# Seven norms of a transformer layer: column sums of width one, or wide sums with a tile of ones

## The chip, the cores and the metric

The kernel runs on one core of a Trainium2 chip. The metric is device time in microseconds. The kernel before takes 1665.77 us, the median of three runs (1663.8, 1665.77 and 1667.88). One further execution was recorded by the profiler: it took 1668.83 us, of which 1665.7 us are the span that the trace covers.

Matrix products run on PE, weights are loaded into it by PEld, elementwise work with two tensors runs on DVE, activations and copies on ACT, a little elementwise work on POOL, and most transfers are issued by SP. Each engine works through its own list of instructions in order; an instruction that waits holds up all that stand behind it on that engine.

## The reference

One encoder layer is applied to two requests with the same weights: a prompt of 512 tokens and a sample of 1024 tokens, both of width 1024, all in fp32. What matters here:

```python
def _rmsnorm(x, g):
    y = x * rsqrt(mean(x * x, axis=-1) + 1e-6) * g

h = _rmsnorm(x, g_pre_mix) * (1 + scale_a) + shift_a
q, k, v, u = split(h @ w_in)
mix = concat(attention(q, k, v), pool(u)) @ w_out
x = x + gate_a * _rmsnorm(mix, g_post_mix)          # the mixer norm
h = _rmsnorm(x, g_pre_mlp) * (1 + scale_m) + shift_m # the norm ahead of feed-forward
x = x + gate_m * _rmsnorm(relu(h @ w_ff1) ** 2 @ w_ff2, g_post_mlp)  # the norm after feed-forward
```

The mean of each norm goes over the 1024 channels of one token.

## The kernel before

Activations are held transposed: a tile has 128 channels on its partitions and 512 tokens along the free dimension, so one half of a request (`c` is 0 for the prompt, 1 for the sample; `hf` is the half, and only the sample has two) is eight such tiles. Since channels lie on partitions, the sum of squares of a token runs across partitions, and PE forms it.

The squares of eight tiles are either added up on DVE first (into `ss`, with the eighth square kept apart as `sq`, so two tiles reach PE), or, in the second norm of the prompt's mixer, handed to PE one by one (eight tiles, there named `x`).

A norm then goes like this. `square_sums` (L195) takes each of the four 128-token slices of a tile as the stationary operand and multiplies it by one column of the tile of ones, so that four matmuls of width one put 512 sums into a 128x4 tile `nv_m`, tokens on partitions. `rsqrt_small` (L163) makes the inverse root of these 128x4 numbers with two activations (`rs_u`, L170 and L171) and four small DVE operations (L172 to L175). `norm_sums` (L177) brings the result back across partitions: four matmuls of 128x128 against the identity write it into `nv_r`, a 128x512 tile in PSUM in which every partition holds the same row (L186), and ACT copies it into SBUF as `nv_R` (L191). With `keep` the copy is left out and the users read PSUM. DVE multiplies the activations by that tile.

The program passes through these stages:

- To about 280 us: the prompt's input projection with its own first norm, the sample's first norms and input projection, the prompt's attention in between.
- From about 290 to 860 us the sample's attention runs in the background. In front of it are the prompt's output projection, the prompt's two mixer norms (`out_post(0, 0)`, 342 to 391 us), and the prompt's feed-forward.
- At 904 us the norm after the prompt's feed-forward (`finish` with `c` 0). The sample's output projection for both halves follows to about 1004 us; `out_post(1, 0)` with its two norms lies inside (953 and 979 us).
- From about 1000 us the sample's first feed-forward product (`ff1_s`), with `out_post(1, 1)` and its two norms (1004 and 1030 us) inside. The second of them is followed by `combine_h`, a long run of elementwise work that makes the operands of a Strassen-like product from both halves.
- To the end: the rest of the feed-forward and the sample's last norms (`finish` with `c` 1), which the change leaves as they are.

A scheduler sets the order in which the instructions of the woven stages stand on each engine. It goes by the order of writing, by priorities and by its own costs. Buffers of a tag are shared in a ring of fixed length: `sq`, `ss` and `nv_R` have two each, the PSUM tile `m` of the norms has one.

Of the kernel before, what the change touches and what calls it, by code (L numbers as in the profile page):

```python
# [7 lines left out]
F32 = mybir.dt.float32  # L8
# [4 lines left out]
AL = mybir.AluOpType  # L13
# [3 lines left out]
KB = 8  # L17
NFB = 32
EPS = 1e-6

V_GPM, V_GQM, V_GPL, V_GQL, V_PS, V_B, V_C = 0, 8, 16, 24, 32, 36, 84
NV = 100
# [24 lines left out]
def hymba_encoder_layer(ctx, tc, xp, xs, ns_, vec, gqk, rope, edge, ident_in, w_ada_c,  # L47
# [129 lines left out]
    def norm_sums(m, keep=False):  # L177

        n = m.shape[1]
        rs = st_p.tile([128, n], F32, tag="nv_rs", name="nv_rs")
        rsqrt_small(rs, m, 1024.0, [128, n], "nv_")
        r = ps_m.tile([128, n * 128], F32, tag="m", name="nv_r")
        for j in range(n):
            nc.tensor.matmul(r[:, j * 128:(j + 1) * 128], lhsT=rs[:, j:j + 1].to_broadcast([128, 128]),  # L186
                             rhs=ident, start=True, stop=True)
        if keep:
            return r
        rt = st_p.tile([128, n * 128], F32, tag="nv_R", name="nv_R")  # L190
        nc.scalar.activation(out=rt, in_=r, func=AF.Copy)  # L191
        return rt

    def square_sums(m, sq, first, last):

        n = m.shape[1]
        for j in range(n):
            nc.tensor.matmul(m[:, j:j + 1], lhsT=sq[:, j * 128:(j + 1) * 128], rhs=ones[:, 0:1],  # L198
                             start=first and j == 0, stop=last and j == n - 1)

    def sums_tile(n=4):
        return ps_m.tile([128, 512], F32, tag="m", name="nv_m")[:, 0:n]

    def norm_vec(sqs, keep=False):

        m = sums_tile(sqs[0].shape[1] // 128)
        for i, sq in enumerate(sqs):
            square_sums(m, sq, i == 0, i == len(sqs) - 1)
        return norm_sums(m, keep)

    def sumsq_add(ss, src, m, eng):

# [546 lines left out]

    def out_post(c, hf):  # L760
        sl = slice(hf * 512, (hf + 1) * 512)
        R = norm_vec(ss_t[c, hf])
        yield
        sqs = []
        if c == 0:
            sums = sums_tile()
        else:
            ss = st_p.tile([128, 512], F32, tag="ss", name="ss2")
        for m in range(KB):
            mx = acc[c, hf][m]  # L770
            xt = land()
            dma(xt, X[c][m, :, sl])
            nc.vector.scalar_tensor_tensor(mx, mx, gg_mix[:, m, c:c + 1], R, op0=AL.mult, op1=AL.mult)
            nc.vector.tensor_tensor(mx, mx, xt, AL.add)
            put(x1_d[c][m, :, sl], mx)
            if c == 0:
                nc.scalar.activation(out=xt, in_=mx, func=AF.Square)
                sqs.append(xt)
                if m > 1:
                    square_sums(sums, sqs[m - 2], m == 2, False)  # L780
            else:
                sq = sumsq_add(ss, mx, m, nc.vector)
            yield
        if c == 0:
            for m in (KB - 2, KB - 1):
                square_sums(sums, sqs[m], False, m == KB - 1)
            R2 = norm_sums(sums)
        else:
            R2 = norm_vec([ss, sq])
        yield  # L790
        if c == 1 and hf == 1:
            yield from combine_h(R2)
            return
        for m, (hh, hl) in enumerate(hi_lo(c, hf)):
            modulate(acc[c, hf][m], R2, a_mlp[:, m, c:c + 1], mod[:, 24 + m, c:c + 1], hh, hl, full=c == 1)
            yield
# [428 lines left out]
    def finish(c, hf, sqs, t0=0, n=512, lands=4):  # L1225
# [8 lines left out]
            dma(xts[m].rearrange("p (m t) -> p m t", m=g), x1_d[c][m:m + g, :, sl].rearrange("m p t -> p m t"))  # L1234
        for m in steps[:lands]:
            load(m)
        R = norm_vec(sqs, True)
        yield
        for m in steps:
            if m not in xts:  # L1240
# [261 lines left out]
```

## Time and profile before

| What | Before |
|---|---|
| median of three runs | 1665.77 us |
| the profiled execution, its own time | 1668.83 us |
| its span in the trace | 1665.7 us |
| PE busy | 1611.2 us, 97% |
| PEld busy | 1299.9 us, 78% |
| DVE busy | 1213.7 us, 73% |
| ACT busy | 854.8 us, 51% |
| mean granted clock of PE | 0.984 |

Busy time is the time in which an engine had an instruction at work. A matmul is recorded with its full length although the next one starts before it ends, so the time that a matmul takes on a busy PE is read from start to start in the timeline, not from its length. A matmul of two fp32 operands is recorded as two instructions, which is why four of them stand as x8. The granted clock is the share of full speed at which PE ran. Waits are put down to the instruction that came last.

### The profile page before, as it was taken

The page shows a single profiled execution, that of the slowest core. Times are in us where ns is not written, and L with a number is a line of the kernel's source. Part 1 is how long each engine was busy: PE and PEld are TensorE (multiplying, and loading weights), DVE is VectorE, ACT ScalarE, POOL GpSimd, SP SyncE. Part 2 cuts the span into 40 slices and gives each one's busy share as a digit, 9 for nine tenths or more (in the row PEclk, how much of TensorE's full clock was granted, in tenths as well). Part 3 has the DMA queues.
Part 4 walks back from the last instruction along what each step waited for, and adds up shares of the span by engine and source line. Part 5 has one row for each costly group of instructions (what it writes and reads, how often), then busy time and mean ns, then how long its engine had stood idle before and what let it go on. Part 6 is the DMA issues. An engine that isn't in the chain of part 4 may idle for free. (4 is left out here: it accounts for less than half of the span.)

```text
span 1665.7 us, 21550 instructions
## 1 busy us (share of the span) xinstructions
PE 1611.2 (97%) x7680; PEld 1299.9 (78%) x7680; DVE 1213.7 (73%) x1938; ACT 854.8 (51%) x1450; POOL 10.4 (1%) x27
## 2 busy tenths in 40 slices
PE   7999998999999999999999999899999999999996
PEld 4467886788888878888888888788888788888886
DVE  7898988568667675655667487878875576878757
ACT  2446664556645545546453475744445564444433
POOL 0000000000000000000000000000000000000002
PEclk8999999989999999999999999999999999999998
DMA  7756776443555553332368537566663745444334
GB/s 294 279 156 186 224 221 183 146 153 123 166 174 180 165 179 102 100 108 89 99 206 245 178 127 246 195 224 226 225 216 121 237 160 186 140 141 152 93 110 152
DMA packets 150618, 287.57 MB, mean 173 GB/s; under 512 B 15152, under 2 KB 56432, under 8 KB 150512
## 3 DMA queue, kind: packets, MB, share of 16 engines
q1 hardware_dynamic: 125824, 258.31, 47.9%
q10 hardware_dynamic: 24688, 27.89, 5.4%
q8 instruction: 60, 0.98, 0.2%
q14 instruction: 46, 0.38, 0.1%
HBM read 223.20 MB, written 61.37 MB: 171 GB/s over the span
## 5 line engine op out<-in xcount | busy, mean ns | idle before, releaser
L140 DVE TENSOR_TENSOR wl<-raw,wh 128x1024 fp32r<-128x1024 f32 (+2 forms) x106 | 121.1, 1142 | 70.4 <-ACT wh L139 69.9
L139 ACT ACTIVATE wh<-raw 128x1024 fp32r<-128x1024 f32 (+2 forms) x106 | 105.4, 995 | 120.4 <-PE mm L160 91.7
L630 ACT ACTIVATE p<-s,amx 128x1024 f32<-128x1024 f32 (+1 forms) x96 | 93.3, 972 | 108.6 <-DVE amx L628 106.7
L657 DVE TENSOR_TENSOR pl<-pT,ph 128x512 fp32r<-128x512 f32 x160 | 108.6, 686 | 54.8 <-ACT ph L656 54.3
L875 PE MATMUL pa<-fo,wh 128*128 128x512 f32 x448 | 140.4, 395 | 2.7 <-ACT x L1012 2.7
L628 DVE TENSOR_REDUCE amx<-s 128x1 f32<-128x1024 f32 (+1 forms) x96 | 100.1, 1042 | 43.5 <-PE s L618 43.1
L656 ACT ACTIVATE ph<-pT 128x512 fp32r<-128x512 f32 x160 | 93.4, 594 | 46.1 <-PE pT L653 36.8
L159 PE MATMUL mm<-hA,wh 128*128 128x512 f32 x256 | 106.7, 417 | 0.0
L159 PE MATMUL mm<-fh,wh 128*128 128x512 f32 x256 | 106.5, 417 | 0.0
L875 PE MATMUL mm<-fo,wh 128*128 128x512 f32 x336 | 104.8, 393 | 0.0
L875 PEld LDWEIGHTS pa<-fo,wh 128*128 128x128 f32 x448 | 84.8, 189 | 21.9 <-ACT x L1012 3.1
L161 PE MATMUL mm<-fh,wl 128*128 128x512 f32 x256 | 101.3, 396 | 0.0
L160 PE MATMUL mm<-fl,wh 128*128 128x512 f32 x256 | 101.0, 394 | 0.0
L160 PE MATMUL mm<-hA,wh 128*128 128x512 f32 x256 | 100.9, 395 | 0.0
L161 PE MATMUL mm<-hA,wl 128*128 128x512 f32 x256 | 100.5, 394 | 0.0
L653 PE MATMUL pT<-ident,p 128*128 128x128 f32 x640 | 96.6, 275 | 1.4 <-DVE pl L657 0.9
L618 PE MATMUL s<-kst,q 128*128 128x512 f32 x320 | 93.9, 406 | 4.0 <-ACT p L630 2.0
L653 PEld LDWEIGHTS pT<-ident,p 128*128 128x128 f32 x640 | 79.3, 142 | 22.6 <-issue 2.4
L875 PE MATMUL pa<-fo,wl 128*128 128x512 f32 x224 | 88.1, 393 | 0.0
L881 ACT ACTIVATE fo<-raw 128x512 fp32r<-128x512 f32 x106 | 66.3, 631 | 38.3 <-DMA raw<-f_d 31.5
L882 DVE TENSOR_TENSOR fo<-raw,fo 128x512 fp32r<-128x512 f32 x106 | 71.2, 689 | 15.8 <-ACT fo L881 15.2
L666 PE MATMUL x<-ph,vst 128*128 128x256 f32 x320 | 81.7, 285 | 0.5 <-ACT ph L656 0.5
(291 smaller groups left out, 3922.5 us busy)
## 6 DMA issues: line engine op xcount, KB each, us to landing
raw<-in_w_ff SPq DMA_DIRECT2D x56, 512.0 KB, 3.8
f_d<-x SPq DMA_DIRECT2D x98, 256.0 KB, 2.8
raw<-f_d SPq DMA_DIRECT2D x98, 256.0 KB, 3.0
raw<-in_w_ada_c SPq DMA_DIRECT2D x40, 512.0 KB, 3.9
g<-in_w_ada_c SPq DMA_DIRECT2D x24, 512.0 KB, 4.3
q<-q_d SPq DMA_DIRECT2D x96, 128.0 KB, 3.6
raw<-in_w_out SPq DMA_DIRECT2D x24, 512.0 KB, 3.8
rawx<-in_w_ff SPq DMA_DIRECT2D x20, 512.0 KB, 4.0
```

Of the source, the lines that this page charges most:

```text
L139: nc.scalar.activation(out=fh, in_=r[:, :n], func=AF.Copy)
L140: nc.vector.tensor_tensor(fl, r[:, :n], fh.bitcast(F32), AL.subtract)
L159: nc.tensor.matmul(ps, lhsT=wh[:, k, :], rhs=ah, start=(i == 0), stop=False)
L160: nc.tensor.matmul(ps, lhsT=wh[:, k, :], rhs=al, start=False, stop=False)
L161: nc.tensor.matmul(ps, lhsT=wl[:, k, :], rhs=ah, start=False, stop=(i == len(ks) - 1))
L618: nc.tensor.matmul(s[:, f * 512:(f + 1) * 512], lhsT=q[:, h, p, :], rhs=kst[c][:, kv, f * 512:(f + 1) * 512].bitcast(F32R), start=(p == 0) ...
L628: nc.vector.tensor_reduce(mx, s[:, :n], AX.X, AL.max, negate=True)
L630: nc.scalar.activation(out=pr, in_=s[:, :n], func=AF.Exp, bias=mx, accum_out=den)
L653: nc.tensor.transpose(t[:, k, :], pr[:, (4 * f + k) * 128:(4 * f + k + 1) * 128], ident)
L656: nc.scalar.activation(out=hi, in_=t, func=AF.Copy)
L657: nc.vector.tensor_tensor(lo, t, hi.bitcast(F32), AL.subtract)
L875: nc.tensor.matmul(ps, lhsT=x[:, k, :], rhs=y, start=start and k == i == 0, stop=k == n - 1 and i == 2, skip_group_check=not start)
```

## The change

Seven norms are formed in another way: both of the prompt's mixer stage (`out_post(0, 0)`), the one after the prompt's feed-forward (`finish` with `c` 0), and the two of each half of the sample (`out_post(1, 0)` and `out_post(1, 1)`). The others keep the old way.

`wide_sums` makes the whole 128x128 tile of ones the stationary operand and streams the tile of squares through PE, 512 columns wide. Each partition of the PSUM tile `nv_w` then holds all 512 sums at once, so nothing has to be brought back across partitions. `wide_norm` makes the inverse root on 128x512 tiles: three activations (Ln, Exp, and an Identity that leaves the mean in SBUF) and three DVE operations, with the same Newton step as before. The result `nv_U` is used where `nv_R` was. These six operations carry a higher priority for the scheduler. The two intermediate tiles come from the ring of `sq`.

```diff
+URGENT = 300
+    def wide_sums(m, sq, first, last):
+        nc.tensor.matmul(m, lhsT=ones, rhs=sq, start=first, stop=last)
+
+    def wide_norm(m):
+        n = m.shape[1]
+        with tc.high_priority(URGENT):
+            u = st_p.tile([128, 512], F32, tag="nv_R", name="nv_U")[:, :n]
+            ms = st_p.tile([128, 512], F32, tag="sq", name="nv_M")[:, :n]
+            t = st_p.tile([128, 512], F32, tag="sq", name="nv_T")[:, :n]
+            nc.scalar.activation(out=u, in_=m, func=AF.Ln, bias=eps_t, scale=1.0 / 1024.0)
+            nc.scalar.activation(out=u, in_=u, func=AF.Exp, scale=-0.5)
+            nc.scalar.activation(out=ms, in_=m, func=AF.Identity, bias=eps_t, scale=1.0 / 1024.0)
+            nc.vector.tensor_tensor(t, u, u, AL.mult)
+            nc.vector.scalar_tensor_tensor(t, t, -0.5, ms, op0=AL.mult, op1=AL.mult)
+            nc.vector.scalar_tensor_tensor(u, t, 1.5, u, op0=AL.add, op1=AL.mult)
+        return u
+
+    def wide_vec(sqs):
+        m = ps_m.tile([128, 512], F32, tag="m", name="nv_w")[:, :sqs[0].shape[1]]
+        for i, sq in enumerate(sqs):
+            wide_sums(m, sq, i == 0, i == len(sqs) - 1)
+        return wide_norm(m)
...
     def out_post(c, hf):
-        R = norm_vec(ss_t[c, hf])
+        R = wide_vec(ss_t[c, hf])
...
-            sums = sums_tile()
+            sums = ps_m.tile([128, 512], F32, tag="m", name="nv_w")
...
-                    square_sums(sums, sqs[m - 2], m == 2, False)
+                    wide_sums(sums, sqs[m - 2], m == 2, False)
...
-                square_sums(sums, sqs[m], False, m == KB - 1)
-            R2 = norm_sums(sums)
+                wide_sums(sums, sqs[m], False, m == KB - 1)
+            R2 = wide_norm(sums)
         else:
-            R2 = norm_vec([ss, sq])
+            R2 = wide_vec([ss, sq])
...
     def finish(c, hf, sqs, t0=0, n=512, lands=4):
-        R = norm_vec(sqs, True)
+        R = norm_vec(sqs, True) if c else wide_vec(sqs)
```

Below the new helpers the line numbers of the changed kernel are 27 higher, so L773 is L800 there, L882 is L909 and L897 is L924.

The change also moves instructions. On PE, in the prompt's mixer stage, the sums of the eight squares `x` stand among the sample's attention (`s`: scores, `pT`: transposed probabilities). Before:

```order
L198 MATMUL nv_m<-ones,x 128x1 x16
L618 MATMUL s<-kst_168,q 128x512 x4
L653 MATMUL pT<-ident,p 128x128 x4
L198 MATMUL nv_m<-ones,x 128x1 x4
L653 MATMUL pT<-ident,p 128x128 x3
L198 MATMUL nv_m<-ones,x 128x1 x4
L653 MATMUL pT<-ident,p 128x128
L666 MATMUL x<-ph,vst_166 128x256
```

and in the change:

```order
L214 MATMUL nv_w<-x,ones 128x512 x4
L645 MATMUL s<-kst_168,q 128x512 x4
L680 MATMUL pT<-ident,p 128x128 x4
L214 MATMUL nv_w<-x,ones 128x512
L680 MATMUL pT<-ident,p 128x128 x4
L214 MATMUL nv_w<-x,ones 128x512 x2
L693 MATMUL x<-ph,vst_166 128x256
```

Sixteen narrow matmuls, the sums of four tiles, have become four wide ones at the same place; the order around them is nearly the same.

On DVE, behind the second norm of the sample's second half, stand the splits of the feed-forward weights (`wl`, L882), each of which PE needs for its next block, and the first operations of `combine_h` (L897). Before:

```order
L1041 TENSOR_TENSOR x<-mm,x 128x512
L882 TENSOR_TENSOR wl<-raw,wh 128x1024
L172 TENSOR_SCALAR nv_ms<-nv_m 128x4
L173 TENSOR_TENSOR rs_t<-rs_u 128x4
L174 SCALAR_TENSOR_TENSOR rs_t<-rs_t,nv_ms 128x4
L175 SCALAR_TENSOR_TENSOR nv_rs<-rs_t,rs_u 128x4
L1041 TENSOR_TENSOR x<-mm,x 128x512
L882 TENSOR_TENSOR wl<-raw,wh 128x1024
L897 TENSOR_TENSOR accA_2909<-accA_2909,nv_R 128x512 x2
```

and in the change:

```order
L909 TENSOR_TENSOR wl<-raw,wh 128x1024
L1068 TENSOR_TENSOR x<-mm,x 128x512
L909 TENSOR_TENSOR wl<-raw,wh 128x1024
L226 TENSOR_TENSOR nv_T<-nv_U 128x512
L227 SCALAR_TENSOR_TENSOR nv_T<-nv_T,nv_M 128x512
L228 SCALAR_TENSOR_TENSOR nv_U<-nv_T,nv_U 128x512
L909 TENSOR_TENSOR wl<-raw,wh 128x1024
L924 TENSOR_TENSOR accA_2909<-accA_2909,nv_U 128x512 x2
```

Counted by weight blocks, one split that stood inside `combine_h` before now stands ahead of it. From the last split shown to the next one lie 21 operations before and 32 in the change; the first read of a product's PSUM tile inside `combine_h` (L1041) was its 16th operation and is now its 20th.

On PE, the same norm's matmuls among the first feed-forward product (`pa` and `mm` are its PSUM tiles) stood like this before:

```order
L198 MATMUL nv_m<-ones,ss_9361 128x1 x4
L875 MATMUL pa<-hA_2904,wh 128x512
L875 MATMUL pa<-hA_2904,wl 128x512
L875 MATMUL pa<-hA_2901,wh 128x512
L198 MATMUL nv_m<-ones,sq 128x1 x4
L875 MATMUL mm<-hA_2905,wh 128x512 x2
L875 MATMUL mm<-hA_2905,wl 128x512
L875 MATMUL mm<-hA_2906,wh 128x512 x2
L875 MATMUL mm<-hA_2906,wl 128x512
L875 MATMUL mm<-hA_2907,wh 128x512 x2
L186 MATMUL nv_r<-ident,nv_rs 128x128 x4
```

and in the change:

```order
L902 MATMUL mm<-hA_2905,wh 128x512
L214 MATMUL nv_w<-ss_9261,ones 128x512
L902 MATMUL mm<-hA_2905,wh 128x512
L902 MATMUL mm<-hA_2905,wl 128x512
L902 MATMUL mm<-hA_2906,wh 128x512 x2
L902 MATMUL mm<-hA_2906,wl 128x512
L214 MATMUL nv_w<-sq,ones 128x512
L902 MATMUL mm<-hA_2907,wh 128x512 x2
```

The sums stand four and six product matmuls later than before, and no matmul of the norm stands behind its DVE operations any more.

## The prediction

> **What bounds the kernel now.** I read the page first, then the granted clock by windows, then PE's waits.
>
> ```profile
> span 1665.7 us, 21550 instructions
> ...
> PE 1611.2 (97%) x7680; PEld 1299.9 (78%) x7680; DVE 1213.7 (73%) x1938; ACT 854.8 (51%) x1450; POOL 10.4 (1%) x27
> ```
>
> PE is busy 97% of the span, so what the norms cost is, first of all, their time on PE. Where PE is slow although busy shows in its clock. Next, windows of 3.4 us around two places where norms lie, all engines; the columns are window, length, busy us of PE, PEld, DVE, ACT and POOL with counts, granted clock, DMA share, GB/s:
>
> ```profile
> 355.00:358.40 3.40, 2.69 (x23) 2.61 (x23) 3.40 (x6) 1.92 (x4) 0.00 (x0) 0.99 0.73 214
> 358.40:361.80 3.40, 3.40 (x14) 3.21 (x14) 3.09 (x6) 1.84 (x3) 0.00 (x0) 0.50 1.03 378
> ...
> 368.60:372.00 3.40, 3.40 (x13) 2.91 (x14) 0.25 (x1) 0.00 (x0) 0.00 (x0) 0.50 0.00 0
> ...
> 1027.40:1030.80 3.40, 2.62 (x19) 2.15 (x18) 2.73 (x4) 1.26 (x2) 0.00 (x0) 1.00 0.68 236
> 1030.80:1034.20 3.40, 3.40 (x11) 2.82 (x11) 1.71 (x6) 2.77 (x6) 0.00 (x0) 0.50 0.77 277
> ...
> 1051.20:1054.60 3.40, 1.84 (x9) 1.16 (x7) 3.40 (x7) 1.74 (x4) 0.00 (x0) 1.00 0.43 147
> 1054.60:1058.00 3.40, 1.98 (x9) 1.63 (x10) 3.40 (x6) 3.01 (x5) 0.00 (x0) 1.00 0.21 78
> ```
>
> and the same for the instructions of `nv_m` alone:
>
> ```profile
> 355.00:358.40 3.40, 2.69 (x23) 2.61 (x23) 0.00 (x0) 0.00 (x0) 0.99 0.73 214
> ...
> 1027.40:1030.80 3.40, 1.61 (x14) 1.74 (x15) 0.00 (x0) 0.00 (x0) 1.00 0.68 236
> ...
> 1051.20:1054.60 3.40, 0.00 (x0) 0.00 (x0) 0.00 (x0) 0.00 (x0) 1.00 0.43 147
> ```
>
> Twice PE runs at half clock, once through the four windows from 358.4 to 372.0 (13.6 us) and once for 3.4 us. Ahead of the first stands a window in which all of PE's 2.69 busy us are sums of width one; ahead of the second one in which 1.61 of 2.62 are. A window with only 1.84 busy us but no such sums (1051.2) is followed by no drop. I take from it that a matmul of width one leaves PE's array nearly idle and counts as idleness for the clock: real work of 0 and of 1.01 us in a window drops it, 1.84 does not. At half clock, 13.6 and 3.4 us of PE's time do the work of 6.8 and 1.7.
>
> Then PE's waits, 330 to 400 us and 895 to 1060 us:
>
> ```profile
> PE nv_m L198 <- ACT x L777: 0.9, 2, 0.6
> ...
> PE pa L875 <- ACT x L1036: 3.0, 1, 3.0
> ...
> PE nv_m L198 <- DVE ss L216: 0.8, 1, 0.8
> ```
>
> Waits are small beside the clock, but for the 3.0 us, in which ACT, busy with `combine_h`, evacuates a product late.
>
> **The prices on PE.** Three pairs of PE timeline rows (start, length), each group and the start of what follows it: four sums of width one; four spreads (`nv_r`); two full fp32 matmuls 512 wide.
>
> ```profile
> 342.06 0.95 PE L198 MATMUL nv_m<-ones,ss 128*128 128x1 f32 x8
> 342.87 0.31 PE L653 MATMUL pT<-ident,p 128*128 128x128 f32 x1
> ...
> 350.28 1.07 PE L186 MATMUL nv_r<-ident,nv_rs 128*128 128x128 f32 x8
> 351.11 1.18 PE L618 MATMUL s<-kst,q 128*128 128x512 f32 x4
> ...
> 61.35 1.88 PE L537 MATMUL mm<-hp,pw 128*128 128x512 f32 x4
> 63.07 1.45 PE L537 MATMUL tb<-hp,pw 128*128 128x512 f32 x3
> ```
>
> From start to start that is 0.81 for a tile's sums, 0.83 for a spread, and 1.72/2 = 0.86 for a wide sum. The seven norms handle 20 tiles: removed 20 x 0.81 + 7 x 0.83 = 22.0, added 20 x 0.86 = 17.2, a gain of 4.8 us on PE at full clock. Per norm of two tiles it is 0.83 - 2 x 0.05 = 0.73.
>
> **The chain off PE.** Before, a norm is two tiny activations, four tiny DVE operations, the spread, and a copy of 0.60; now three activations and three DVE operations of full width. Rows of the prompt's stage, DVE, ACT and PE apart:
>
> ```profile
> 347.67 0.16 DVE L172 TENSOR_SCALAR nv_ms<-nv_m 128x4 f32<-128x4 f32 x1 [0.78 <-ACT rs_u L170]
> ...
> 352.02 1.42 DVE L773 SCALAR_TENSOR_TENSOR accA<-accA,gg_mix,nv_R 128x512 f32<-128x512 f32 x2 [1.35 <-ACT nv_R L191]
> ...
> 365.41 0.68 DVE L774 TENSOR_TENSOR accA<-accA,x 128x512 f32<-128x512 f32 x1
> ...
> 371.75 1.23 DVE L628 TENSOR_REDUCE amx<-s 128x1 f32<-128x1024 f32 x1 [5.06 <-PE s L618]
> ...
> 377.05 2.08 DVE L223 SCALAR_TENSOR_TENSOR accA<-accA,a_mlp,nv_R 128x512 f32<-128x512 f32 x3 [0.79 <-ACT nv_R L191]
> ...
> 347.38 0.26 ACT L170 ACTIVATE rs_u<-nv_m,eps_t 128x4 f32<-128x4 f32 x1 [1.21 <-PE nv_m L198]
> ...
> 351.39 0.60 ACT L191 ACTIVATE nv_R<-nv_r 128x512 f32<-128x512 f32 x1 [0.81 <-PE nv_r L186]
> ...
> 366.63 0.62 ACT L777 ACTIVATE x<-accA 128x512 f32<-128x512 f32 x1
> ...
> 372.08 0.95 PE L198 MATMUL nv_m<-ones,x 128*128 128x1 f32 x8
> ```
>
> The wide chain is 3 x 0.6 on ACT and about 0.7 + 0.7 + 0.7 on DVE, some 3.9 us from the last sum to the first user; before it was 352.02 - 347.38 = 4.6 us, since two short steps stood behind attention's DVE work and the spread waited in PE's list. So the first norm's users start within half a microsecond of where they did. Per norm DVE gains 2.1 - 0.6 = 1.5 us of work, ACT 1.8 - 1.1 = 0.7 (estimates from these rows).
>
> **The prompt's mixer stage (342 to 377 us).** The users of the first norm start at about 352.0 as before, and DVE's order behind them is the same, so its last L774 still starts at about 365.4 and the last square ends at 366.63 + 0.62 = 367.3. Before, PE at half clock came to that square's sums only at 372.08 and left them at about 372.9. If the clock stays up, PE waits for DVE, takes the last square at 367.3 and is done at 368.2. Its second norm's users then start at 368.2 + 3.9 + a little queueing, about 372.5, instead of 377.05. This stage gains **4.5 us**. Its PE account is 6.8 (clock) + 2 x 0.83 - 10 x 0.05 = 8.0, so some 3.5 us go into new waits for DVE; following the new order by these durations I find the least busy window at about 1.7 us, of wide work, near the 1.84 that held.
>
> **Three norms under cover (904, 953 and 979 us).**
>
> ```profile
> 895.00:985.00 90.00, 90.00 (x423) 73.33 (x422) 57.59 (x88) 39.63 (x63) 0.00 (x0) 1.00 0.59 198
> ```
>
> PE never stops here while DVE is busy 57.6 of 90 us and ACT 39.6, so the wider vector work is hidden (were it not, 1.5 us a norm on DVE) and PE's saving is the gain: 3 x 0.73 = **2.2 us**.
>
> **The sample's second half (1004 and 1030 us).** PE saves 2 x 0.73, the wait of 0.8 for `ss` (the sum now stands four matmuls later), and 1.7 of clock: 4.0 us by the time `combine_h` begins. Then DVE bounds. Rows of DVE's timeline:
>
> ```profile
> 1036.25 2.50 DVE L897 TENSOR_TENSOR accA<-accA,nv_R 128x512 f32<-128x512 f32 x4 [1.26 <-ACT nv_R L191]
> ...
> 1045.29 0.69 DVE L1041 TENSOR_TENSOR x<-mm,x 128x512 f32<-128x512 f32 x1
> ```
>
> `combine_h` starts at about 1036 either way, for a weight split more stands ahead of it now, and the L1041 that frees PE's bank is its 20th operation instead of its 16th: 4 x 0.6 = 2.4 later, near 1047.7. PE arrives early and waits some 5 us there, but holds ten more product matmuls behind it; the next split comes about 3 us earlier than its fellow did, and the wait of 3.0 behind ACT has less cause. I give back 1.7 of the 4.0: **2.3 us**, with bounds of 0.5 (nothing but PE's removed work less a longer wait) and 5 (the 3.0 us wait gone too).
>
> **Sum.** 4.5 + 2.2 + 2.3 = 9.0. The profiled execution, 1668.8 us with 3.1 around its span, becomes 1659.8; it lay 3.1 above the median, so the median becomes **1657 us**. The order elsewhere changes by a few rows only; I cost that at nothing, with 1.5 either way for a half-clock window that falls differently.
>
> **Rivals.**
>
> *The clock drops all the same.* The half clock could come from the stage's pauses or from PE's slow feed by DVE, which the change keeps. Then the prompt's stage gains only its spreads less the wider sums, 1.1, the sample's 1.4, with 2.2 under cover: 4.7, so 1661. For it: PE will pause more in this stage than before. Against it: the window at 1051.2, busy for 1.84 us, held the clock. The Trainium skill, "TensorE: Matmul & The Clock Gate", section "HAM oscillation — how this bites in real kernels", asks for idle gaps above about 3.4 us before the clock falls, and speaks so for this rival: by it the drop here, with waits of 0.6 us at the longest ahead of it, is not caused by pauses, and nothing in it says that the change would end it. The trace agrees that pauses alone are not the cause: the drop follows a window that the profile calls busy for 2.69 of 3.4 us.
>
> *The gain is given back to DVE.* PE leaves each norm earlier only to wait for weights and exponentials. If both open stages end where they did, 2.2 remain: 1664. For it: DVE is busy 3.40 of 3.40 in windows of both stages. Against: before, DVE itself stood still for 5.06 us up to 371.75, waiting for PE.
>
> *Slower: DVE becomes the bound at all seven norms.* The wide operations go ahead of attention's and the weights' work. Place: the vector engine's list at each norm; price 7 x 1.5 = 10.5 us, plus 5 of wait at 1042 to 1048 and the clock as before, less the 4.8 on PE: 10.7 slower, so 1676; it decides against the change once over half of that lands on PE's path. Against: 57.6 of 90 us around three of the norms.
>
> *More gain.* If the waits inside `combine_h` go altogether, 4.8 more: 1652.
>
> That the change does not do what it says is excluded: the new order has the 20 wide sums and no spread in these seven norms.
>
> **How the numbers follow.** The forecast gets 0.57, the kept half clock 0.13, the gain given back 0.12, slower 0.08, more gain 0.10. A change of 0.3% (5 us) is about what can be told from none here. Faster by that: nearly all of the forecast (0.53), the larger gain (0.10) and a third of the half-clock case (0.04): 0.67. Slower 0.08. The rest, 0.25, is the same. The likeliest case spans 1652 to 1661; taking in the neighbours on both sides the range is 1649 to 1666.
>
> **What would show it.** Right: the clock at 1.00 from 355 to 372 us; wide sums of two records 0.43 apart; first users of the prompt's second norm near 372.5; PE without waits at 895 to 985 and about 2 us further by its end; a wait of some 5 us near 1043 for L1068. Wrong: a clock of 0.50 in the prompt's stage, PE waiting at the three covered norms, or those users no earlier than 376.

## The result, and the profile after

The changed kernel takes 1657.2 us (median of 4 executions, 1655.8 to 1658.1) where the kernel before takes 1664.9 beside it (median of 4). The ratio is 0.9941, with a 95% interval of 0.9925 to 0.9957: 7.7 us or 0.6% faster. The profiled execution took 1656.99 us, 11.8 less than the profiled one of before; 10.6 of these lie in the span. A second comparison (below) gave 0.9947 (0.9932 to 0.9962).

The predicted time was 1657. The parts of its sum, though, did not come out as predicted, and most of what follows is about that.

The page of the changed kernel: span, and busy time of each engine.

```profile
span 1655.1 us, 21193 instructions
...
PE 1598.6 (97%) x7504; PEld 1275.7 (77%) x7504; DVE 1222.4 (74%) x1931; ACT 860.3 (52%) x1451; POOL 10.4 (1%) x27
```

PE's busy time fell by 12.6 us, more than the span; a part of that is the same work done at full clock. DVE has 8.7 us more to do, ACT 5.5.

The stretches of 3.4 us around the two places of the prediction, all engines (window, length, busy us of PE, PEld, DVE, ACT, POOL, granted clock, DMA share, GB/s):

```profile
355.00:358.40 3.40, 2.01 (x5) 0.68 (x4) 3.40 (x6) 2.03 (x4) 0.00 (x0) 1.00 0.71 198
358.40:361.80 3.40, 2.59 (x7) 1.20 (x8) 3.40 (x5) 2.11 (x5) 0.00 (x0) 1.00 0.78 297
...
368.60:372.00 3.40, 3.40 (x21) 2.48 (x20) 1.82 (x2) 1.73 (x4) 0.00 (x0) 1.00 0.33 106
...
1034.20:1037.60 3.40, 0.00 (x0) 0.00 (x0) 3.35 (x7) 3.40 (x7) 0.00 (x0) 0.97 0.00 0
1037.60:1041.00 3.40, 0.30 (x1) 0.30 (x2) 3.40 (x7) 3.40 (x7) 0.00 (x0) 0.50 0.00 0
```

The prompt's stage keeps a clock of 1.00, with PE busy for as little as 2.01 us of 3.4. A new half clock stands behind 1037, after a stretch in which PE did nothing at all. PE's waits, 330 to 400 us and then 895 to 1060 us, say why (us in all, times, longest):

```profile
PE nv_w L214 <- ACT x L804: 1.7, 3, 1.2
PE pT L680 <- DVE pl L684: 1.3, 2, 0.8
...
PE mm L902 <- DVE x L1068: 6.5, 1, 6.5
PE pa L902 <- DVE wl L909: 0.9, 2, 0.5
```

Timeline rows of the prompt's stage, DVE, ACT and PE apart (start, length), which answer to those of before:

```profile
352.96 1.41 DVE L800 SCALAR_TENSOR_TENSOR accA<-accA,gg_mix,nv_U 128x512 f32<-128x512 f32 x2
...
366.72 0.68 DVE L801 TENSOR_TENSOR accA<-accA,x 128x512 f32<-128x512 f32 x1
...
375.21 2.07 DVE L250 SCALAR_TENSOR_TENSOR accA<-accA,a_mlp,nv_U 128x512 f32<-128x512 f32 x3
...
367.94 0.62 ACT L804 ACTIVATE x<-accA 128x512 f32<-128x512 f32 x1
...
370.73 0.69 ACT L223 ACTIVATE nv_U<-nv_w,eps_t 128x512 f32<-128x512 f32 x1 [1.68 <-PE nv_w L214]
...
369.66 1.02 PE L214 MATMUL nv_w<-x,ones 128*128 128x512 f32 x2
```

The second norm's users start at 375.21, against 377.05 before and 372.5 predicted.

**Where the time came from.** Each of the 7384 matmuls that PE's trace records outside the norms occurs in both profiles, so the n-th of a line and a pair of operands in one can be laid beside the n-th in the other. The difference of their start times shows how far the changed kernel is ahead at each place. The table gives that lead for the profile of the change, for a second profile of it, and for the experiments that follow (us, against the one profile of before; the clock's windows, below, make single executions differ by a few us).

| lead at the place | change | change, second profile | prompt only | covered three only | last two only |
|---|---|---|---|---|---|
| 340 us, ahead of the prompt's stage | -0.7 | -3.0 | 0.1 | 0.8 | 0.9 |
| 400 us | 2.2 | -0.1 | 2.9 | 0.6 | 0.9 |
| 895 us | 5.5 | 1.4 | 6.2 | 0.8 | 2.0 |
| 1000 us, behind the covered three | 8.9 | 4.9 | 6.3 | 4.2 | 2.0 |
| 1075 us | 9.2 | 5.6 | 6.0 | 0.5 | 4.9 |
| 1600 us | 10.6 | 6.8 | 6.8 | 1.0 | 5.2 |

So in the first pair of profiles the prompt's stage gave 2.9 (predicted 4.5), the stretch from 400 to 895 us 3.3 (predicted nothing), the covered norms 3.4 (predicted 2.2), the sample's second half 0.3 (predicted 2.3), and 1.4 came behind 1075, where a stretch of half clock at 1328 is missing in the profile after. The 2.9 of the prompt's stage comes again in every profile that has the change's norms there (2.7 to 2.9 in five). The 3.3 behind it does not belong to the change as surely: four profiles that keep the old norms in the prompt's stage show 0.2, 1.1, 1.1 and 3.0 there against the same profile of before (covered three, last two, and the two kernels of experiment 2).

### The profile page after: what moved, and what is told of

It reads as the page before. It is cut to its first block, busy times and chain, and to the rows that moved or that the text cites. A ratio compares the mean times of both kernels' runs of the same rounds, so it can differ in the third digit from the quotient of the medians.

```text
span 1655.1 us, 21193 instructions
## 1 busy us (share of the span) xinstructions
PE 1598.6 (97%) x7504; PEld 1275.7 (77%) x7504; DVE 1222.4 (74%) x1931; ACT 860.3 (52%) x1451; POOL 10.4 (1%) x27
## 5 line engine op out<-in xcount | busy, mean ns | idle before, releaser
L694 PE MATMUL x<-pl,vst 128*128 128x256 f32 x320 | 81.1, 286 | 1.2 <-DVE pl L684 1.2
```

## The experiments

### 1. Does a narrow product count as idleness? (64 and 128 columns)

In the kernel before, the prompt's mixer norms form their sums against `cols` columns of ones instead of one. The price on PE and the work of all other engines stay.

```diff
-            nc.tensor.matmul(m[:, j:j + 1], lhsT=sq[:, j * 128:(j + 1) * 128], rhs=ones[:, 0:1],
+            c = m[:, j * cols:(j + 1) * cols]
+            nc.tensor.matmul(c, lhsT=sq[:, j * 128:(j + 1) * 128], rhs=ones[:, 0:cols],
...
-        R = norm_vec(ss_t[c, hf])
+        R = norm_vec(ss_t[c, hf], cols=1 if c else 64)
...
-            sums = sums_tile()
+            sums = sums_tile(256)
```

> The kernel before, with the prompt's two mixer-stage norms summing against 64 columns of ones in place of one (four narrow products per tile as before; 63 copies of each sum are never read). PE's order stays as before but for one spread that stands a few products later; the four tiles of sums that stand in a row stay in a row. Theory 1 (a matmul of width one leaves the array idle, and that drops the clock): the clock stays at 1.00 from 355 to 372 us, the second norm's users start near 373.5 in place of 377.05, and the kernel gains 3 to 4 us there: about 1661.5 against 1665. Theory 2 (pauses and the slow feed by the vector engine drop the clock, whatever the width): 0.50 from about 358 to 372 as before, and 1665 within 1. Theory 3 (it needs a fuller array than 64 of 128 columns): 0.50 as before here and 1.00 with 128 columns.

> The same with 128 columns of ones (the 127 copies are never read). PE's price of a tile's sums should stay at 0.81 to 0.83 us, the price of the spread, which is also four matmuls 128 wide. The scheduler now sets the tiles of sums apart from one another instead of four in a row. Theory 1 (width): clock at 1.00 from 355 to 372, gain 3 to 4 us, 1661.5. Theory 2 (pauses, feed): 0.50 in that stretch, 1665 within 1. Theory 3: 1.00 here though 0.50 with 64 columns.

64 columns: 1666.0 us, ratio 0.9988 (0.9973 to 1.0003). 128 columns: 1666.0, ratio 0.9980 (0.9965 to 0.9996). The kernel before took 1668.7 beside them. It took 1667.8, 1665.7 and 1666.1 in the later groups of runs, so only times of one group, or ratios, can be compared. The stage, all engines, with 64 columns and then with 128:

```profile
355.00:358.40 3.40, 2.35 (x17) 2.16 (x18) 3.40 (x7) 2.12 (x4) 0.00 (x0) 0.85 0.62 191
358.40:361.80 3.40, 3.40 (x17) 3.40 (x18) 3.04 (x5) 2.15 (x4) 0.00 (x0) 0.50 0.99 306
361.80:365.20 3.40, 3.40 (x18) 2.91 (x18) 3.39 (x6) 1.64 (x4) 0.00 (x0) 0.64 0.78 254
```

```profile
355.00:358.40 3.40, 2.83 (x26) 2.62 (x24) 2.09 (x3) 1.09 (x2) 0.00 (x0) 1.00 0.93 353
358.40:361.80 3.40, 3.21 (x23) 2.99 (x24) 3.40 (x7) 2.73 (x6) 0.00 (x0) 1.00 0.69 201
```

One column gave 13.6 us at half clock, 64 columns 6.8, 128 none: a matter of degree, between theories 1 and 3. But with 128 columns the scheduler had also set the tiles apart, so the pair alone does not prove it. Laid beside the profile of before, product by product as in the table above, the stage itself gained 2.4 and 3.6 us (3 to 4 expected). It did not stay: with 64 columns it was lost to half clock at 419, 600 and 1054, and with 128 a lead of 6.0 at 850 became 3.8 by the end, most of the loss at a half clock at 1322. The clock evidently falls in many places, and differently from one execution to the next.

### 2. The same question where PE never waits

The kernel before, with the sums of the covered norm at 904 us done six times over, against one column and against 128.

```diff
-        for i, sq in enumerate(sqs):
+        for i, sq in list(enumerate(sqs)) * reps:
...
-        R = norm_vec(sqs, True)
+        R = norm_vec(sqs, True, 1 if c else 1, 1 if c else 6)
```

(the last two arguments are the columns and the repetitions; the other kernel has `1 if c else 128` for the columns)

> The kernel before, with the narrow sums of one covered norm (904 us) done six times over: twelve tiles of four products of width one, eleven of them in a row on PE, the same sums each time. PE has 10 x 0.81 = 8.1 us more to do there and never waits. Theory 1 (the clock is set, window by window of 3.41 us, by how much of a window the array streams columns; a narrow product streams one column in 0.1 us): at least one whole window is without streaming though PE is busy all the time, so the clock, 1.00 there in every execution so far, falls to 0.50 within 907 to 912 for two or three windows; the stretch costs 8.1 plus 2 to 5 us. Theory 2 (waits and pauses drop the clock): PE has none, the clock stays at 1.00 from 895 to 985, the cost is 8.1.

> The same twelve tiles with 128 columns of ones in place of one (127 copies are never read), at the same 0.81 to 0.83 us a tile. Theory 1: the array streams all the while, the clock stays at 1.00, and the stretch costs 8.3 us. Theory 2: 1.00 as well, 8.3; only the pair of runs tells them apart. If the clock fell here too, it would be the fp32 products as such, or the change between kinds of product, that drop it.

Each ran once, under the profiler. Windows of 5 us, all engines, with one column:

```profile
900.00:905.00 5.00, 5.00 (x42) 4.77 (x41) 1.46 (x2) 0.96 (x2) 0.00 (x0) 1.00 0.83 267
905.00:910.00 5.00, 5.00 (x29) 5.00 (x28) 0.00 (x0) 0.00 (x0) 0.00 (x0) 0.58 0.49 190
910.00:915.00 5.00, 5.00 (x25) 5.00 (x25) 0.00 (x0) 0.00 (x0) 0.00 (x0) 0.50 0.00 0
915.00:920.00 5.00, 5.00 (x19) 4.52 (x20) 0.65 (x4) 0.47 (x2) 0.00 (x0) 0.50 0.00 0
```

and with 128:

```profile
905.00:910.00 5.00, 5.00 (x47) 5.00 (x46) 1.39 (x2) 0.00 (x0) 0.00 (x0) 1.00 0.56 181
...
910.00:915.00 5.00, 4.90 (x28) 3.90 (x27) 2.81 (x8) 0.47 (x2) 0.00 (x0) 1.00 0.00 0
```

With one column PE works through without a gap, with 128 it pauses for 0.1 us at the end. With one column the clock falls to 0.50; with 128, the same twelve tiles in the same place, it stays at 1.00. By the lead at 895 and 925 us the ten added tiles cost 16.7 us with one column and 9.0 with 128 (expected 10 to 13, and 8.3). The first is more than expected because narrow products at half clock take twice as long (0.21 us from one record to the next instead of 0.11) and are still narrow, so the clock stays down for 17 us instead of two or three windows. **Theory 1 is shown, theory 2 has fallen**: it is not PE's idleness but the lack of streaming.

**The rule that all fourteen profiles follow.** The trace's record of the granted clock changes only at moments that lie whole multiples of 3.413 us apart, at an offset that is different in each execution (before: half clock from 279.84 to 286.67, 358.35 to 372.00, 1030.77 to 1034.19, 1327.73 to 1331.14). I took each such window and added up the time in which the array streams columns: the columns of each product at 0.42 ns, and 0.83 ns for each record of an fp32 product or a transpose; twice that at half clock. Both figures are estimates from dense rows: fp32 products of 512 columns follow each other every 0.43 us, the other products every 0.23 us with 512 columns and every 0.12 with 256. Some windows, with PE's busy share beside it:

| execution | window from | PE busy | streaming | clock of the next window |
|---|---|---|---|---|
| six times, one column | 902.4 | 1.00 | 0.01 | 0.50 |
| before | 354.9 | 0.77 | 0.01 | 0.50 |
| before | 1027.4 | 0.77 | 0.25 | 0.50 |
| 128 columns | 1021.6 | 0.81 | 0.29 | 0.50 |
| 64 columns | 354.0 | 0.66 | 0.33 | 0.50 |
| prompt only | 297.6 | 0.42 | 0.37 | 0.50 |
| root without refinement | 1013.1 | 0.46 | 0.38 | 1.00 |
| before | 1051.2 | 0.52 | 0.44 | 1.00 |
| the change | 347.9 | 0.63 | 0.46 | 1.00 |

Between 40 and 1640 us the fourteen executions have 6465 windows at full clock. The 53 that are followed by half clock stream for 0.37 of the window or less; the 6412 that are followed by full clock, for 0.385 or more. From half clock, 50 windows led back to full, each streaming for 0.78 or more; 48 did not, each at 0.74 or less. There is no exception. PE's busy share does not separate them: 1.00 fell, 0.46 held. Transposes have to be counted: without them, windows down to 0.21 would be among those that held. The limits go by the two estimates per column.

The Trainium skill, "TensorE: Matmul & The Clock Gate", section "Part 1: The HAM clock gate (the "warmup" mystery)", states free-running windows of 3413 ns, with which these traces agree. The same page of the Trainium skill, section "HAM oscillation — how this bites in real kernels", has the clock fall after idle gaps of PE above some 3.4 us; here it fell without a gap (PE busy 1.00 of the window at 902.4 us), and the measurement decides.

Since the windows run free, a short narrow or slow stretch is caught in some executions and not in others. The one in the prompt's stage is not short: in the profile of before, windows that start from 353.2 to 354.9 us, half of the possible offsets, stream under 0.385 and end before the clock falls at 358.35. That is a lower bound, since behind 358.35 the profile shows only the stage at half clock; all five profiles with the narrow sums there fall to half clock for 13.6 to 17.1 us. With 128 columns a fifth of the offsets would still have found a window at 0.31 to 0.38 there, from about 348 us. In both profiles of the change no offset finds one in this stage (0.44 at the least).

### 3. The change in parts

The change in two of the seven norms (the prompt's), in three (finish at 904, the sample's first half at 953 and 979), and in two (the sample's second half):

```diff
-        R = wide_vec(ss_t[c, hf])
+        R = norm_vec(ss_t[c, hf]) if c else wide_vec(ss_t[c, hf])
...
-            R2 = wide_vec([ss, sq])
+            R2 = norm_vec([ss, sq])
...
-        R = norm_vec(sqs, True) if c else wide_vec(sqs)
+        R = norm_vec(sqs, True)
```

(the prompt only; the others have the conditions `(c, hf) == (1, 0)` and `(c, hf) == (1, 1)` in the same lines)

> The change in the prompt's mixer norms alone (two of the seven). Theory 1, the prediction's sum: 4.5 us, 1660.4. Theory 2, the two traces laid side by side: 2.9 us up to 400 us, another 3.3 between 400 and 600 us where attention and the prompt's feed-forward meet another phase of one another, less 0.7 of scatter ahead of the stage: 5.5, 1659.4, and nothing gained at 895 to 1060. Theory 3: the 3.3 belong to chance of one execution and stay away: 1662. Clock at 1.00 from 355 to 372 in all.

> The change in the three norms at 904, 953 and 979 us alone. Theory 1, the prediction's term of 0.73 each: 2.2 us, 1662.7. Theory 2, PE's rows: entering and leaving the narrow groups costs PE another 0.4 us a norm, so 1.1 to 1.2 each: 3.4, 1661.5, reached by about 985 us and unchanged until 1000. The prompt's stage keeps its drop to 0.50. Theory 3 (the wider vector work shows): under 1.5, with PE waiting between 895 and 985.

> The change in the sample's second half alone (norms at 1004 and 1030 us). Theory 1, the prediction's term: 2.3 us faster than the kernel before. Theory 2, from the two traces laid side by side: PE gains about 1.2 per norm by 1030 us and gives all of it back in a wait of some 6 us for L1068, so 0 to 0.5 us, with the prompt's stage at its old clock. Theory 3: the wait and the clock that falls after it cost more than the norms save: 1 to 3 us slower.

Prompt only: 1659.8 us, ratio 0.9948 (0.9926 to 0.9969). Covered three: 1665.3, ratio 0.9982 (0.9968 to 0.9996). Last two: 1661.8, ratio 0.9967 (0.9953 to 0.9982). The means over all executions, against those of the kernel before on the same chip, can be split: (1 - granted clock) x span is the time lost to the clock (it counts the slow start and the slow end of the program too, alike in all), the remainder is PE's work and waits. Differences in us, each with its standard error; the clock is known to 0.001, so the split is good to about 1 us.

| kernel (executions) | time | lost to the clock | the rest |
|---|---|---|---|
| prompt only (8) | -8.5 ± 1.1 | -10.2 ± 0.8 | +1.7 ± 0.7 |
| covered three (12) | -2.7 ± 0.9 | +1.3 ± 1.0 | -4.1 ± 0.7 |
| last two (12) | -5.6 ± 1.0 | -2.0 ± 0.9 | -3.5 ± 0.7 |
| 64 columns (12) | -2.4 ± 0.9 | -3.7 ± 0.9 | +1.3 ± 0.6 |
| 128 columns (12) | -2.8 ± 0.9 | -6.9 ± 1.1 | +4.1 ± 0.9 |
| the change (6) | -9.0 ± 1.2 | -6.5 ± 1.2 | -2.5 ± 1.2 |

The prompt's two norms alone bring nearly as much as the whole change, and by the clock. Theory 2's time of 1659.4 was met, but by luck: it expected a gain of 5.5 us, and beside the kernel before it was 8.5. The 3.3 us between 400 and 895 are there again in this profile (2.9 to 6.2), 1.5 in the second profile of the change; but the profiles with the old norms there have 0.2 to 3.0, so how much of it the change causes is not shown. It lies where attention and the feed-forward meet: before, PE waited there for the softmax's weights at 420 and 598 us (rows of before, 400 to 440 and 580 to 612):

```profile
PE dT L644 <- DVE pl L657: 1.6, 1, 1.6
...
PE s L618 <- ACT p L630: 1.6, 1, 1.6
```

The three covered norms give 3.4 us by 985 (0.8 to 4.2), as theory 2 said. At 1075 the lead of this profile is 0.5, but that is the clock: it has half clock from 1027.1 to 1033.9 and from 1054.4 to 1057.8 us where the profile of before has only 1030.8 to 1034.2, and 6.8 us more at half clock are 3.4 us lost. Over its executions the gain is 2.7 ± 0.9, between theories 1 and 2. The last two norms alone give 5.6, which none of the three theories expected (2.9 between 1000 and 1075 in its own profile), where the profiles of before and after had shown 0.3 for this place. The gains of the parts add up to 16.8, the whole has 9.0, so they take from each other. By the leads, part of it happens in the sample's second half: behind 1000 us the change gains 0.3 and 0.7 in its two profiles, the last two norms alone 2.9. There PE's first product and the start of `combine_h` on DVE, for the change and then for the last two norms alone:

```profile
991.65 0.64 PE L902 MATMUL pa<-hA,wh 128*128 128x512 f32 x2
...
1023.24 1.22 DVE L909 TENSOR_TENSOR wl<-raw,wh 128x1024 fp32r<-128x1024 f32 x1 [2.06 <-ACT wh L908]
...
1026.98 1.22 DVE L909 TENSOR_TENSOR wl<-raw,wh 128x1024 fp32r<-128x1024 f32 x1
1028.11 3.09 DVE L924 TENSOR_TENSOR accA<-accA,nv_U 128x512 f32<-128x512 f32 x5
```

```profile
998.49 0.39 PE L902 MATMUL pa<-hA,wh 128*128 128x512 f32 x1
...
1030.35 2.50 DVE L924 TENSOR_TENSOR accA<-accA,nv_U 128x512 f32<-128x512 f32 x4
...
PE pa L902 <- DVE wl L909: 3.7, 1, 3.7
```

With the covered norms wide, `combine_h` starts 36.5 us behind the first product; without them 31.9 (before the change 35.7, by the same two rows). The wait of 6.5 us for L1068 is then gone, with 3.7 for a weight split in its place.

The difference is in DVE's list, not in the norms' work, which between these two rows is the same in both kernels. The change has three more weight splits of 1.22 us ahead of `combine_h` (seven start between the two rows instead of four); DVE is busy there for 29.2 us instead of 25.3, and idle for 7.3 and 6.5. Over all fourteen profiles the start goes with this count: four splits ahead, 31.5 to 32.1 us; five (the old way in the sample's half and in the covered norms), 33.7 to 36.4; seven, 36.1 to 36.9. Covered three alone has six, and 38.5 with its two more windows at half clock. A split that does not stand ahead of `combine_h` stands inside it; with the last two alone PE waits its 3.7 us for such a one.

### 4. The wait of 6.5 us: place in the list, or arrival?

The evacuation for which PE waits is put ahead in the scheduler's order:

```diff
-                nc.vector.tensor_tensor(c11, ps, s[1], AL.add)
+                with tc.high_priority(URGENT if early else 0): nc.vector.tensor_tensor(c11, ps, s[1], AL.add)
```

> All of the change, and the vector engine's evacuation L1068 of the second product (the operation for which PE waits 6.5 us at 1033 to 1040) put ahead in the scheduler's order: it becomes the 16th operation behind combine_h's start again, as before the change, in place of the 20th. Theory 1 (the wait is the place in the vector engine's order): 4 x 0.6 = 2.4 us shorter, and the half clock that follows it gone in most executions: 2 to 4 us faster than the change, so 10 to 12 faster than before. Theory 2 (combine_h's own work bounds this place): PE waits as long one product later, and nothing changes: 7.5 to 8 faster than before.

1658.4 us, ratio 0.9944 (0.9926 to 0.9962), 9.4 ± 0.9 us by the means beside the change's 9.0 ± 1.2: not clearly faster than the change. PE's wait:

```profile
PE mm L902 <- DVE x L1068: 4.8, 2, 4.5
PE pa L902 <- DVE wl L909: 1.8, 2, 1.1
PE pa L902 <- ACT x L1063: 1.6, 1, 1.6
```

The longest wait shrank by 2.0, about the 4 x 0.6 expected, and came back as 0.9 more for weight splits and 1.6 for ACT. Theory 2 holds: while `combine_h` starts this late, the stretch lasts as long in either order (from the first product to one that comes 69 us behind it before the change: 68.5 with the change, 69.4 here, 65.7 with the last two alone). In wide_norm itself the priority moves nothing: with URGENT at 0 the lists of PE, DVE and ACT are the same.

### 5. Without the covered norms; with a shorter chain

Three kernels: the prompt's and the last two norms only; all seven with the root straight from logarithm and exponential; all seven with the square of the refinement on ACT. Beside them the change itself.

```diff
-            nc.vector.tensor_tensor(t, u, u, AL.mult)
+            nc.scalar.activation(out=t, in_=u, func=AF.Square)
```

(the third; the second leaves out nv_M, nv_T and the four lines from `out=ms` on)

> The changed kernel as it is, timed beside the next two on one chip, and a second profile of it with another phase of the clock's windows. Expected 8 to 10 us faster than the kernel before, a clock of 1.00 all through the prompt's stage in this execution too, and a wait of 6 to 7 us for L1068 before the clock may or may not fall behind it (by the first profile's streaming, in 4 executions of 10).

> The change in the prompt's two norms and the sample's last two, without the three covered ones. Theory 1 (the three covered norms cost as much as they bring: the vector engine comes into the sample's second half later by their wider work, so that combine_h starts some 4.6 us later behind the first product there): the gains of the two parts add, 8.5 and 5.6, the wait at L1068 is gone or under 2 us, combine_h starts 32 to 33 us behind the first product in place of 36.5, and the kernel is 12 to 14 faster than before, 3 to 5 faster than the change. Theory 2 (PE's own gain of 3.3 there counts): 3 slower than the change, 5 to 6 faster than before.

> All seven norms wide, but with the reciprocal root straight from the logarithm and the exponential: the refinement step (one activation and three operations of the vector engine per norm) is left out, so this version computes the root less exactly. Per norm 2.1 us less of the vector engine and 0.7 of ACT. Theory 1 (the wider vector work is what holds the sample's second half and the prompt's stage back): combine_h starts at most 33 us behind the first product there, the wait at L1068 under 3 us, PE waits under 3 in the prompt's stage in place of 5.7, and the kernel is 4 to 7 faster than the change. Theory 2 (vector work is covered but for its place in the order): within 2 of the change.

> All of the change with the refinement kept, but its square u*u made by ACT in place of the vector engine: per norm one vector operation of 0.69 us fewer and one activation of 0.6 more, with the same sums on PE. Theory 1 (the vector engine's work per norm delays the sample's second half; without three operations a norm combine_h started 5.0 us sooner behind the first product there): a third of it, combine_h at 34 to 35 us behind the first product in place of 36.5, PE's wait at L1068 4 to 5 us, 0.5 to 2 us faster than the change, 9.5 to 11 faster than before. Theory 2 (the length of the chain counts, whatever engine does it): combine_h at 36 to 36.5, PE's wait 6 to 7, the change's time within 0.5.

| kernel | median us | ratio to before (95%) | combine_h behind the first product | PE's longest wait there |
|---|---|---|---|---|
| the change | 1657.6 | 0.9947 (0.9932 to 0.9962) | 36.1 | 6.5 for L1068 |
| prompt's and last two | 1658.5 | 0.9956 (0.9940 to 0.9971) | 31.9 | 3.7 for a weight split |
| no refinement | 1654.8 | 0.9931 (0.9917 to 0.9945) | 31.5 | 3.3 for `ss` |
| square on ACT | 1657.5 | 0.9937 (0.9917 to 0.9956) | 32.1 | 3.8 for a weight split |

Rows of the second and third kernel, waits from 985 to 1080 us (the second row is DVE's):

```profile
PE pa L902 <- DVE wl L909: 3.7, 1, 3.7
DVE x L1076 <- DMA x<-s_d: 3.2, 1, 3.2
PE pc L902 <- DVE x L1076: 2.3, 1, 2.3
```

```profile
PE nv_w L214 <- DVE ss L237: 3.3, 1, 3.3
```

The second profile of the change has the wait of 6.5 us for L1068 again, and the clock falls behind it in both. That was expected in 4 executions of 10 only. But the wait is longer than a window of 3.413 us: windows that start from 1032.7 to 1038.5 us in the first profile stream for 0.37 or less, and that is more than one window's length, so no offset would have missed it.

Without the covered norms, `combine_h` started as early as expected, but the kernel was not 3 to 5 us faster than the change; it was the same. Its lead of 8.7 us at 1075 (places of the profile of before) fell to 4.8 by 1090: at 1077 to 1079 us of its own time PE waited 2.3 us for a reload from memory that DVE had waited 3.2 for, and the clock fell behind it. The kernel with the last two alone has the same lists from there on and no such wait; this reload landed 5.8 us after its issue, where 3.9 is the median of its kind. Why it was late is open. But it does not explain the missing 3 to 5 us: the profiled execution took 1662.3 us, four of the other five 1657.1 to 1659.1, still no faster than the change. And even ahead of that wait its lead of 8.7 was no more than the change's, 9.2 in its first profile and, 3.0 behind already at 340, 5.6 in its second. What the three covered norms bring, 3.4 us by 1000, and what they take in the sample's second half were about equal here.

Without the refinement the median is the lowest of all, 10.9 us under before. Beside the change it is 2.8 lower, with intervals that overlap, where 4 to 7 had been expected. PE's waits in the prompt's stage come to 3.3 us in place of 5.7. With the square on ACT `combine_h` starts 4.0 us sooner behind the first product, nearly as much as with three operations fewer, so it does not go by the amount of vector work as theory 1 had it. All three kernels, the one without the covered norms too, have four weight splits ahead of `combine_h`, where the change has seven. None of the runs moved a split alone, so that the splits are the cause rests on this count. The time with the square on ACT cannot be told from the change's (1657.5 and 1657.6). Both of these profiles show half clock in or just ahead of the prompt's stage (351 to 354 and 354 to 360 us) although the sums are wide: PE's waits there brought streaming to 0.31 and 0.28 of a window. Wide sums keep the clock only as long as PE has something to stream.

## Why the prediction was right in the sum and wrong in its parts

- **The half clock comes of narrow products: right, and shown.** In the stage the clock was 1.00 in both profiles of the change. "Twice PE runs at half clock" was a miscount, though: between 40 and 1640 us the profile of before has four such stretches, also from 279.84 and from 1327.73. The explanation was a step short: "real work" in a window, 0 and 1.01 against 1.84 us of 3.4, stands for the streaming share, and the limit lies between 0.37 and 0.385.
- **The prompt's stage, 4.5: mis-sized.** 2.9 in the pair of profiles. The failed step is "takes the last square at 367.3 and is done at 368.2. Its second norm's users then start at 368.2 + 3.9". The stage began 0.7 later (the lead of -0.7); the last L801 ran at 366.72 instead of 365.41; the last square ended at 368.56, and its sum started only at 369.66 behind products of attention in PE's list; and the chain to the first user took 375.21 - 370.52 = 4.7 instead of 3.9, since an attention step stands between the six. Over many executions the same two norms gave 8.5 us, with 10.2 less lost to the clock, in this stage (6.8 in the profile of before) and in others; which others is not shown.
- **Nothing elsewhere in the order, 1.5 either way: wrong in the pair of profiles by the 3.3 us at 400 to 895.** The prompt's wide norms alone show them too, but profiles with the old norms reach 3.0, so this may be scatter that the term made too small.
- **Three covered norms, 3 x 0.73 = 2.2: mis-sized at 985, where it is 3.4.** PE's rows around the norm at 904 us, before and then after:

```profile
903.80 0.95 PE L198 MATMUL nv_m<-ones,ssf 128*128 128x1 f32 x8
904.61 0.48 PE L159 MATMUL mm<-oh,wh 128*128 128x512 f32 x1
904.92 0.95 PE L198 MATMUL nv_m<-ones,sq 128*128 128x1 f32 x8
905.73 0.48 PE L160 MATMUL mm<-ol,wh 128*128 128x512 f32 x1
906.05 0.39 PE L161 MATMUL mm<-oh,wl 128*128 128x512 f32 x1
906.28 0.39 PE L159 MATMUL mm<-oh,wh 128*128 128x512 f32 x1
...
906.75 0.39 PE L161 MATMUL mm<-oh,wl 128*128 128x512 f32 x1
907.14 1.13 PE L186 MATMUL nv_r<-ident,nv_rs 128*128 128x128 f32 x8
908.03 0.48 PE L159 MATMUL mm<-oh,wh 128*128 128x512 f32 x1
908.34 0.39 PE L160 MATMUL mm<-ol,wh 128*128 128x512 f32 x1
```

```profile
898.23 1.02 PE L214 MATMUL nv_w<-ssf,ones 128*128 128x512 f32 x2
899.09 1.02 PE L214 MATMUL nv_w<-sq,ones 128*128 128x512 f32 x2
899.55 0.79 PE L160 MATMUL mm<-oh,wh 128*128 128x512 f32 x1
900.18 0.40 PE L161 MATMUL mm<-ol,wh 128*128 128x512 f32 x1
```

A product between products takes 0.23 from start to start (906.05 to 906.28). Next to the narrow groups three products take 0.31, one 0.39, and the spread itself 0.89: 2 x 0.81 + 0.89 + 3 x 0.08 + 0.16 = 2.91. After, the two sums and the product behind them last 900.18 - 898.23 = 1.95, less that product's own 0.23: 1.72. The gain is 1.19 a norm, not 0.73; the groups' borders were missing from the price. "The wider vector work is hidden" held where it is done:

```profile
895.00:985.00 90.00, 90.00 (x377) 70.34 (x376) 64.47 (x91) 47.90 (x72) 0.00 (x0) 1.00 0.58 188
```

Alone, the three norms brought 2.7 ± 0.9 us by the end, close to the term. Beside the other wide norms they brought little (the change's median is 0.9 us under that of the kernel without them). What the term left out is not the vector work but the order: in the change, two more weight splits than before stand ahead of `combine_h` in the next stage, and three more than without these norms.
- **The sample's second half, 2.3: mis-sized.** 0.3 and 0.7 in the two profiles of the change, 5.6 over the executions when changed alone. "4.0 us by the time `combine_h` begins" was right: the lead rises from 8.9 at 1000 us to 13.0 at 1040. The failed step is "I give back 1.7 of the 4.0": by 1075 the lead is 9.2, so 3.8 are given back (3.7 in the second profile). The wait "of some 5 us near 1043 for L1068" came as 6.5 at 1034 to 1041, and the two windows at half clock behind it, 3.4 us, had no price. The reason given, "its 20th operation instead of its 16th", accounts for 2 us of the wait at most. "Starts at about 1036 either way" held within the stage: 36.5 us behind the first product instead of 35.7.
- **The rivals.** The clock did not drop all the same: it is 1.00 from 340 to 400 us in all five profiles that have the change's norms there. That the gain is given back to DVE was nearly right for the sample's second half and wrong for the prompt's. Slower did not happen.

So the time of 1657 is partly luck, because the errors cancelled: 4.5 + 2.2 + 2.3 = 9.0 was 2.9 + 3.4 + 0.3 in the profiles, with 3.3 and 1.4 from places that had been costed at nothing and -0.7 ahead.

## What to carry to other kernels

Price a matmul by two numbers, its time on PE and the time in which columns stream: here narrow products cost as much as products 128 wide, and a row of them halved the clock of what followed. Look for stretches where streaming falls below 0.4 of any 3.4 us, and read more than one execution, because the windows run free. A change of one stage can give the scheduler another order in the next: compare the lists there too, above all what stands ahead of the operation for which the busiest engine waits. The lead of one profile over the other, product by product, shows where a gain is made and where it is lost; profiles of kernels that are alike up to a place show how much of it is scatter.

## What the runs showed of the hardware that I had not expected

- The clock follows the streaming share of free-running windows of 3.413 us: it fell after 0.37 or less, held from 0.385 on, and came back after 0.78 or more and not after 0.74 or less, without an exception in fourteen executions. Transposes count as streaming.
- Half clock feeds itself: twelve tiles of narrow products kept the clock down for 17 us, and the ten of them that had been added cost 16.7 us where the same ten, 128 wide, cost 9.0.
- A change between kinds of product costs PE 0.08 to 0.16 us at each border (0.31 and 0.39 instead of 0.23 from start to start).
